# Sums of squares by one-column products in PSUM, and ScalarE scaling in the first layer's attention

## The chip, the core and the metric

The kernel runs on one core of a Trainium2 chip. A core has five engines that run side by side, each through its own queue in order: TensorE (PE, matrix products into PSUM), VectorE (DVE), ScalarE (ACT), GpSimd (POOL) and SyncE (SP, which here issues transfers). The metric is the device time of one execution in microseconds, as a median of several.

## What is computed

A decoder trunk of two layers on 512 prompt tokens and 8 sequences of 4 new tokens, all in float32, 544 columns in all. Cut to what matters here:

```
h  = rms_norm(x) * (1 + scale1(c)) + shift1(c)     # mean of squares over 1024 features
q  = rotary(rms_norm(q by heads)); k likewise      # mean of squares over 64 features of a head
p  = exp(s - m) / (sum exp(s - m) + exp(sink - m)) # attention in a window of 128, with sinks
o  = concat(rms_norm(o_attn), rms_norm(o_ssm), rms_norm(o_lru)) @ w_o
x  = x + gate1(c) * o
h2 = rms_norm(x) * (1 + scale2(c)) + shift2(c)
x  = x + gate2(c) * ConvFFN(h2)
```

The scales, shifts and gates come from c by a product with w_ada, a matrix of 1024 by 6144 for each layer.

## The kernel before

Features lie on the 128 partitions (1024 features are 8 chunks), tokens on the columns, and the columns are worked in two halves: half 0 has tokens 0 to 255, half 1 tokens 256 to 511 and the 32 new ones. A scheduler orders each engine's instructions at build time: in the order of the program, but what it reckons to be ready earlier may go first. `tc.keep_in_program_order` ties one instruction behind the one written before it on its engine.

**Stages.** The head (to about 66 us of the trace) loads x and the weights, computes the modulation and the first norm. Each layer then has mixers (to about 300 us, and from 700 to 933) and a feed-forward stage. In the head and the mixers, slabs of w_ada of 512 KB arrive through three buffers `raw`, which the weights share; PE multiplies each slab (L524, eight passes) and so sets its buffer free for the next transfer that SP has in its queue. Weights come through the same buffers, are split by ACT (`whi`, L415) and DVE (`wlo`, L416), and are multiplied in three passes (L430). Between these products PE takes small ones for attention, SSM and LRU, which ticks of hand-written generators interleave.

**Norms.** A norm needs, for every token, a sum of squares over features, that is over partitions and chunks. ACT squares the chunks; `sq_accum` adds them on DVE into one tile `sqacc` (L837). `mean_rstd` transposes it on PE in two blocks of 128 tokens (L459), so that tokens lie on partitions, and DVE reduces the columns (L465); the new tokens are summed by a product with a matrix of ones (L463). `rstd_small` takes the parts, scales each (L385), and finds the inverse root in eight further steps on DVE. `spread` transposes the result back to all partitions (L478), ACT copies it (L845), and the chunks are multiplied by it (L856). The head calls `sq_accum` for half 0 before its first slab and for half 1 before its ninth (`SQN`), and the statistics after two and after twelve slabs (`S12`), each pinned in PE's order.

The norms at the ends of stages have their squares added as the chunks come out of the residual. `head_rstd` does the same for each of five tiles of q and k in a layer: four transpositions (L931), a reduction over groups of 64 columns (L933), and a product with a block matrix of ones, `bones` (L936). `out_norm` adds two tiles of squares for SSM and LRU (L1126) before the same steps. The tiles of squares come from four buffers `half`.

**Attention.** A unit is one pair of heads by 128 queries, 16 units in a layer. `att_S` copies the sinks into the tile of scores (L1241), multiplies q and k (L1242), masks and finds the maximum (L1244), ACT takes exponentials with their sum, DVE the reciprocal (L1251) and scales two tiles of 256 or 128 columns (L384). PE transposes the result (L1263) and multiplies it by v (L1277).

Of the kernel before, what the change touches and what calls it, by code (L numbers as in the profile page):

```python
# [316 lines left out]
def trunk(ctx: ExitStack, tc: tile.TileContext, A, O):  # L317
# [130 lines left out]
    def mean_rstd(hfs, n, squares, pin=False):  # L448


        nb = 2 * len(hfs)
        m = nb + (32 if 1 in hfs else 0)
        c = sp.tile([128, 4], F32, tag="cs", name="cs", bufs=2)
        parts, held = [c[:, 0:nb]], []
        for i, hf in enumerate(hfs):
            sq = squares(hf)
            ps = one(256 + 32 * hf)
            for j in range(2):
                z = T_.transpose(ps[:, 128 * j:128 * j + 128], sq[:, 128 * j:128 * j + 128], eye)  # L459
                if pin and not i and not j:  # L460
                    tc.keep_in_program_order(z)
            if hf:
                T_.matmul(ps[:, 256:288], ones, sq[:, 256:288], start=False, stop=True, skip_group_check=True)  # L463
                parts.append(ps[:, 256:288])
            V.tensor_reduce(c[:, 2 * i:2 * i + 2], ps[:, 0:256].rearrange("p (j n) -> p j n", j=2),  # L465
                            axis=AX.X, op=OP.add)
            held.append(ps)
        r = sp.tile([128, 40], F32, tag="qr", name="qr", bufs=3)
        rstd_small(parts, n, r[:, 0:m])
        for ps in held:  # L470
            PS.put(ps)
        return r[:, 0:nb], r[:, nb:m]

    def spread(r, pin=False):
# [351 lines left out]

    SQ = {}

    def sq_accum(c, hf):
        a, b = HALF[hf]  # L830
        if c == 0:
            SQ[hf] = sp.tile([128, 288], F32, tag=f"sqacc{hf}", name="sqacc", bufs=1)[:, :b - a]
            act(SQ[hf], x[:, c, a:b], AF.Square)
        else:
            s = W(b - a)
            act(s, x[:, c, a:b], AF.Square)
            V.tensor_add(SQ[hf], SQ[hf], s)  # L837

    def norm_stats(hf, pin=False):

        r, rs = mean_rstd((hf,), 1024, lambda hf: SQ[hf], pin)
        yield
        ps = spread(r, pin)
        nr = SQ[hf]
        S.copy(nr[:, 0:256], ps)  # L845
        if hf:
            V.tensor_copy(nr[:, 256:288], rs)
        PS.put(ps)
# [77 lines left out]
            S.dma_start(dst[32 * i:32 * i + 32], src[o:o + 32])  # L926

    def head_rstd(M, sq):
        pt = one()
        for j in range(4):  # L930
            T_.transpose(pt[:, 128 * j:128 * j + 128], sq[:, 128 * j:128 * j + 128], eye)  # L931
        c = sp.tile([128, 8], F32, tag="ch", name="ch", bufs=2)
        V.tensor_reduce(c, pt.rearrange("p (n f) -> p n f", f=64), axis=AX.X, op=OP.add)  # L933
        PS.put(pt)
        pr = one(32)
        T_.matmul(pr, M.bones, sq[:, NP:NT], start=True, stop=True)  # L936
        r = sp.tile([128, 40], F32, tag="hr", name="hr", bufs=4)
        rstd_small((c, pr), 64, r)
        PS.put(pr)
        return r  # L940

    def k_chain(l, M, ps):
# [173 lines left out]
    def out_norm(l, M, os, at, n, hfs=(0, 1)):  # L1116
        d = LY[l]
        w = slice(HALF[hfs[0]][0], HALF[hfs[-1]][1])

        def squares(hf):  # L1120
            if not at:
                return M.sq.pop(hf)
            t = [W(HALF[hf][1] - HALF[hf][0]) for _ in os]
            for z, o in zip(t, os):
                act(z, o[:, slice(*HALF[hf])], AF.Square)
            V.tensor_add(t[0], t[0], t[1])  # L1126
            return t[0]

        r, rs = mean_rstd(hfs, n, squares)
        yield 1  # L1130
        nr = spread(r)
        a, b = w.start, min(w.stop, NP)
        for i, o in enumerate(os):
            wo = d["won"][at + i]
            stt(o[:, a:b], o[:, a:b], wo, nr, OP.mult, OP.mult)
            if 1 in hfs:
                stt(o[:, NP:NT], o[:, NP:NT], wo, rs, OP.mult, OP.mult)
        PS.put(nr)
        while not M.win_done:
            yield 1  # L1140
        for i, o in enumerate(os):
            split(o[:, w], [z[:, w] for z in hs[at + i]])
            M.o.update((at + i, hf) for hf in hfs)
            if at:
                free(o)
# [86 lines left out]
    def att_S(l, M, u):  # L1232
# [5 lines left out]
        pv = ps.rearrange("p (g n) -> p g n", g=2)  # L1238
        pm = M.pool.tile([128, 2, 257], F32, tag="pm", name="pm", bufs=PMB)
        st = sp.tile([128, 3, 2], F32, tag="st", name="st", bufs=4)  # L1240
        V.tensor_copy(pm[:, :, nk:nk + 1], d["nsink"][:, c, :, None])  # L1241
        T_.matmul(pv, M.q[c][:, j * 128:j * 128 + 128], M.kz[:, :, k0:k0 + nk], start=True, stop=True)  # L1242
        for g in range(2):
            V.tensor_tensor_reduce(out=pm[:, g, 0:nk], in0=pv[:, g], in1=M.maskp[:, 256 - nk:256],  # L1244
# [5 lines left out]
                accum_out=st[:, 1, g:g + 1])  # L1250
        V.reciprocal(st[:, 2], st[:, 1])  # L1251
        for g in range(2):
            ts(pm[:, g, 0:nk], pm[:, g, 0:nk], st[:, 2, g:g + 1])
        return pm

    def att_T(l, M, u, pm):
# [481 lines left out]
    for l in range(L):  # L1738
        with tc.tile_pool(name=f"mix{l}", bufs=1, reuse_waits="tile") as pool, ExitStack() as stack:
# [6 lines left out]
            if l == 0:  # L1746
# [13 lines left out]
                for n in range(24):  # L1760
                    if n == S3:
                        W_.ahead(GRP)
                        fetch_x(1)
                    for hf in range(2):
                        if n == SQN[hf]:
                            for c in range(KC):
                                sq_accum(c, hf)
                    for at, g in zip(S12, st + st):
                        if n == at:
                            next(g, None)  # L1770
# [41 lines left out]
```

## Time and profile before

| what | value |
|---|---|
| median of 3 runs | 1332.7 us (1332.39 to 1332.75) |
| the profiled execution | 1335.0 us, its span 1333.2 us |
| TensorE's granted clock, mean | 0.992 of full |
| PE busy | 1270.1 us, 10438 instructions |
| DVE busy | 881.8 us, 2583 instructions |
| ACT busy | 576.5 us, 1112 instructions |
| read from HBM | 159.37 MB |

The span runs from the first to the last instruction on record; the time of the execution includes what lies around it. PE's busy time counts overlapping passes once and is modelled at its ends. In the rows, L463 is line 463; `out<-in` names what is written and read; `x8` counts instructions; what stands in brackets is the engine's idle time before the row and what ended it.

### The profile page before, as it was taken

What the parts mean: (1) busy time and instruction counts of PE and PEld (TensorE: products, weight loads), DVE (VectorE), ACT (ScalarE), POOL (GpSimd) and SP (SyncE); (2) the same over time, 40 slices, a digit from 0 to 9 for tenths busy, and PEclk for the clock granted to TensorE, in tenths of its full rate; (3) what the DMA queues carried; (4) which work ended last, traced back from release to release, by engine and by line L of the source; (5) the groups of instructions that cost most, each with busy time, mean ns of one, the idle gap of its engine ahead of it and who ended that gap; (6) DMA issues with size and microseconds to landing.
All of it is one profiled execution on the core that took longest, in us unless ns stands there. A gap on an engine that the chain in (4) does not pass through costs nothing.

```text
span 1333.2 us, 26368 instructions
## 1 busy us (share of the span) xinstructions
PE 1270.1 (95%) x10438; PEld 1164.8 (87%) x10438; DVE 881.8 (66%) x2583; ACT 576.5 (43%) x1112; POOL 48.8 (4%) x82
## 2 busy tenths in 40 slices
PE   4899988999999999999999999899999999999998
PEld 2666765799999999999998776679999999999998
DVE  8787885988774556456576877668865456545651
ACT  4557544356542343234354466545643234313430
POOL 0021010000020000000000001000000000000000
PEclk9899999999999999999999999999999999999999
DMA  8876677533343223334235846602322332233221
GB/s 294 279 265 215 191 252 229 178 111 118 93 135 125 85 86 87 97 93 115 76 108 180 268 142 203 191 14 90 110 81 86 96 95 74 86 97 94 85 72 51
DMA packets 72460, 178.24 MB, mean 134 GB/s; under 512 B 15584, under 2 KB 26752, under 8 KB 72336
## 3 DMA queue, kind: packets, MB, share of 16 engines
q1 hardware_dynamic: 65456, 162.08, 39.1%
q0 software_dynamic: 4960, 11.68, 2.5%
q10 hardware_dynamic: 1920, 2.79, 0.7%
q8 instruction: 82, 1.34, 0.4%
q14 instruction: 42, 0.34, 0.1%
HBM read 159.37 MB, written 14.34 MB: 130 GB/s over the span
## 4 chain that ended last, share of the span: by engine, by line
PE 83%; DMA 9%; DVE 5%; ACT 2%; issue 1%; POOL 0%; SPq 0%; DVEq 0%; POOLq 0%; ACTq 0%
PE wide L430 42%; PE fb1w L430 9%; PE fb0w L430 8%; DMA raw<-in_wada_dram 6%; PE fb0s L430 5%; PE fb1s L430 4%; PE mb0s L430 3%; PE mb1s L430 3%; PE mb0s L524 1%; PE mb1s L524 1%; DMA raw<-in_wo_dram 1%; DVE wlo L416 1%; DMA f<-in_ssmh_dram 1%; DMA tab_br<-f 1%; PE mb1s L1242 0%
## 5 line engine op out<-in xcount | busy, mean ns | idle before, releaser
L430 PE MATMUL wide<-hh,whi 128*128 128x288 f32 (+1 forms) x1360 | 400.3, 295 | 1.2 <-ACT hh L897 0.8
L430 PE MATMUL wide<-hl,whi 128*128 128x288 f32 (+1 forms) x1360 | 395.9, 291 | 0.0
L430 PE MATMUL wide<-hh,wlo 128*128 128x288 f32 (+1 forms) x1360 | 394.3, 290 | 0.0
L416 DVE TENSOR_TENSOR wlo<-raw,whi 128x1024 fp32r<-128x1024 f32 (+1 forms) x176 | 211.0, 1200 | 187.1 <-ACT whi L415 183.1
L415 ACT CAST whi<-raw 128x1024 fp32r<-128x1024 f32 (+1 forms) x176 | 180.4, 1029 | 274.8 <-PE wide L430 125.8
L430 PEld LDWEIGHTS wide<-hh,whi 128*128 128x128 f32 x1360 | 257.2, 189 | 18.3 <-issue 14.0
L430 PEld LDWEIGHTS wide<-hl,whi 128*128 128x128 f32 x1360 | 257.1, 189 | 6.3 <-issue 6.1
L430 PEld LDWEIGHTS wide<-hh,wlo 128*128 128x128 f32 x1360 | 259.2, 191 | 3.0 <-issue 3.0
L380 DVE SCALAR_TENSOR_TENSOR f<-wide,prm,f 128x511 f32<-128x511 f32 x236 | 100.2, 485 | 0.0
L430 PE MATMUL wide<-mid,whi 128*128 128x256 f32 (+1 forms) x526 | 99.8, 287 | 0.0
L430 PEld LDWEIGHTS wide<-mid,whi 128*128 128x128 f32 x526 | 82.4, 188 | 0.0
L897 ACT CAST mid<-f 128x544 fp32r<-128x544 f32 x44 | 28.5, 647 | 122.4 <-DVE f L1660 119.1
L430 PE MATMUL wide<-mid,wlo 128*128 128x256 f32 (+1 forms) x263 | 75.5, 287 | 0.0
L377 ACT ACTIVATE f<-f 128x544 f32<-128x544 f32 x50 | 33.0, 659 | 89.2 <-DVE f L1650 84.5
L430 PE MATMUL fb1w<-hh,whi 128*128 128x256 f32 (+1 forms) x240 | 69.4, 289 | 1.8 <-ACT hh L862 1.3
L430 PE MATMUL fb1w<-hl,whi 128*128 128x256 f32 (+1 forms) x240 | 69.4, 289 | 0.0
L430 PE MATMUL fb1w<-hh,wlo 128*128 128x256 f32 (+1 forms) x240 | 68.8, 287 | 0.0
L430 PE MATMUL fb0w<-hh,whi 128*128 128x256 f32 (+1 forms) x224 | 64.7, 289 | 1.6 <-ACT hh L862 1.1
L430 PE MATMUL fb0w<-hl,whi 128*128 128x256 f32 (+1 forms) x224 | 64.7, 289 | 0.0
L430 PE MATMUL fb0w<-hh,wlo 128*128 128x256 f32 (+1 forms) x224 | 64.3, 287 | 0.0
L430 PE MATMUL fb0s<-mid,whi 128*128 128x288 f32 (+1 forms) x326 | 62.9, 290 | 0.0
L430 PE MATMUL fb1s<-mid,whi 128*128 128x288 f32 (+1 forms) x308 | 59.1, 289 | 0.0
(612 smaller groups left out, 2542.2 us busy)
## 6 DMA issues: line engine op xcount, KB each, us to landing
raw<-in_wada_dram SPq DMA_DIRECT2D x92, 512.0 KB, 5.2
raw<-in_wup_dram SPq DMA_DIRECT2D x88, 512.0 KB, 3.5
raw<-in_wdn_dram SPq DMA_DIRECT2D x32, 448.0 KB, 3.3
raw<-in_win_dram SPq DMA_DIRECT2D x24, 512.0 KB, 4.2
raw<-in_wo_dram SPq DMA_DIRECT2D x16, 512.0 KB, 4.5
raw<-in_wdn_dram SPq DMA_DIRECT2D x16, 512.0 KB, 3.5
e<-q ACTq DMA_DIRECT2D x32, 68.0 KB, 4.6
out_ox_dram<-x SPq DMA_DIRECT2D x8, 272.0 KB, 2.1
```

Of the source, the lines that this page charges most:

```text
L377: return S.activation(out, in_, f, bias=bias, scale=scale, **kw)
L380: return V.scalar_tensor_tensor(out, a, s, b, op0=op0, op1=op1, **kw)
L415: S.copy(hi, raw)
L416: V.tensor_sub(lo, raw, f32(hi))
L430: T_.matmul(out, w[wi][:, k, :], r[ri][:, a:b], start=first and i == 0, stop=last and i == 2)
L524: T_.matmul(ps[32 * g:32 * g + 32], silu[:, k, :], have[n][:, g], start=k == 0, stop=k == 7, skip_group_check=True)
L897: S.copy(dst[0], src)
```

## The change

Sums over features are now made by products in which the squares are the stationary operand and one column of ones moves; the result has tokens on partitions, as after a transposition, with the sum done. All products of a norm go into different columns of one PSUM tile and add up there, so several tiles of squares need no addition before. The first product of the tile clears it. In the head the squares are made when the norm asks for them (`sq_start`), one buffer each, and all eight chunks are multiplied; there is no `sq_accum` and no `SQN` in the head any more. The norms at the ends of stages still add their squares on DVE. `head_rstd` uses two columns of `bones` instead of a transposition and a reduction. In layer 0 alone, the copy of the sinks and the scaling of the probabilities are done on ACT.

```diff
@@ mean_rstd
-        c = sp.tile([128, 4], F32, tag="cs", name="cs", bufs=2)
-        parts, held = [c[:, 0:nb]], []
+        ps = one(m)
+        first = True
         for i, hf in enumerate(hfs):
-            sq = squares(hf)
-            ps = one(256 + 32 * hf)
-            for j in range(2):
-                z = T_.transpose(ps[:, 128 * j:128 * j + 128], sq[:, 128 * j:128 * j + 128], eye)
-                if pin and not i and not j:
-                    tc.keep_in_program_order(z)
-            if hf:
-                T_.matmul(ps[:, 256:288], ones, sq[:, 256:288], start=False, stop=True, skip_group_check=True)
-                parts.append(ps[:, 256:288])
-            V.tensor_reduce(c[:, 2 * i:2 * i + 2], ps[:, 0:256].rearrange("p (j n) -> p j n", j=2),
-                            axis=AX.X, op=OP.add)
-            held.append(ps)
+            for sq in squares(hf):
+                for j in range(2):
+                    z = T_.matmul(ps[:, 2 * i + j:2 * i + j + 1], sq[:, 128 * j:128 * j + 128], ones[:, 0:1],
+                                  start=first, stop=True, skip_group_check=True)
+                    if pin and first:
+                        tc.keep_in_program_order(z)
+                    first = False
+                if hf:
+                    T_.matmul(ps[:, nb:m], ones, sq[:, 256:288], start=False, stop=True, skip_group_check=True)
         r = sp.tile([128, 40], F32, tag="qr", name="qr", bufs=3)
-        rstd_small(parts, n, r[:, 0:m])
+        rstd_small([ps], n, r[:, 0:m])
@@ norms
+    def sq_start(hf):
+
+        a, b = HALF[hf]
+        SQ[hf] = sp.tile([128, 288], F32, tag=f"sqacc{hf}", name="sqacc", bufs=1)[:, :b - a]
+        for c in range(KC):
+            s = W(b - a)
+            act(s, x[:, c, a:b], AF.Square)
+            yield s
-        r, rs = mean_rstd((hf,), 1024, lambda hf: SQ[hf], pin)
+        r, rs = mean_rstd((hf,), 1024, lambda hf: [SQ[hf]] if hf in SQ else sq_start(hf), pin)
@@ head_rstd
-        pt = one()
+        ps = one(40)
         for j in range(4):
-            T_.transpose(pt[:, 128 * j:128 * j + 128], sq[:, 128 * j:128 * j + 128], eye)
-        c = sp.tile([128, 8], F32, tag="ch", name="ch", bufs=2)
-        V.tensor_reduce(c, pt.rearrange("p (n f) -> p n f", f=64), axis=AX.X, op=OP.add)
-        pr = one(32)
-        T_.matmul(pr, M.bones, sq[:, NP:NT], start=True, stop=True)
+            T_.matmul(ps[:, 2 * j:2 * j + 2], sq[:, 128 * j:128 * j + 128], M.bones[:, 0:128:64],
+                      start=j == 0, stop=True, skip_group_check=True)
+        T_.matmul(ps[:, 8:40], M.bones, sq[:, NP:NT], start=False, stop=True, skip_group_check=True)
-        rstd_small((c, pr), 64, r)
+        rstd_small([ps], 64, r)
@@ out_norm, squares
-                return M.sq.pop(hf)
+                return [M.sq.pop(hf)]
-            V.tensor_add(t[0], t[0], t[1])
-            return t[0]
+            return t
@@ att_S
-        V.tensor_copy(pm[:, :, nk:nk + 1], d["nsink"][:, c, :, None])
+        (V.tensor_copy if l else S.copy)(pm[:, :, nk:nk + 1], d["nsink"][:, c, :, None])
-            ts(pm[:, g, 0:nk], pm[:, g, 0:nk], st[:, 2, g:g + 1])
+            z = pm[:, g, 0:nk]
+            if l:
+                ts(z, z, st[:, 2, g:g + 1])
+            else:
+                act(z, z, AF.Copy, scale=st[:, 2, g:g + 1])
@@ the head
-                    for hf in range(2):
-                        if n == SQN[hf]:
-                            for c in range(KC):
-                                sq_accum(c, hf)
```

## Rows read from the trace of the kernel before

**Rows 1.** Busy time of each engine by stretch, clock, DMA share, GB/s.

```profile
66.00:133.00 67.00, 61.65 (x534) 45.77 (x527) 53.89 (x220) 43.70 (x102) 13.55 (x24) 1.00 0.74 238
...
500.00:600.00 100.00, 100.00 (x801) 100.00 (x801) 54.53 (x110) 30.88 (x47) 0.00 (x0) 1.00 0.31 92
700.00:890.00 190.00, 175.19 (x1497) 136.17 (x1496) 139.56 (x470) 103.20 (x234) 9.47 (x12) 0.99 0.57 175
```

**Rows 2.** The page: busy time of the engines; chain of waits by engine.

```profile
PE 1270.1 (95%) x10438; PEld 1164.8 (87%) x10438; DVE 881.8 (66%) x2583; ACT 576.5 (43%) x1112; POOL 48.8 (4%) x82
...
PE 83%; DMA 9%; DVE 5%; ACT 2%; issue 1%; POOL 0%; SPq 0%; DVEq 0%; POOLq 0%; ACTq 0%
```

**Rows 3.** Chain of waits from 66 to 262 us, shares by line.

```profile
by line: PE wide L430 19.0%; DMA raw<-in_wada_dram 17.8%; PE mb0s L524 7.5%; DMA raw<-in_wo_dram 7.1%; PE mb0s L430 6.3%; DMA f<-in_ssmh_dram 4.4%; DMA tab_br<-f 3.5%; PE mb0s L1081 2.7%; PE mb0s L1263 2.2%; PE mb0s L1242 2.2%; issue 2.1%; 
```

**Rows 4.** One piece of that chain in the head: start, us.

```profile
8.68 0.41 DVE sqacc L837
```

**Rows 5.** PE's timeline, three slabs of w_ada: start, us, [idle before].

```profile
13.94 1.08 PE L524 MATMUL wide<-raw,cin 128*32 128x256 f32 x8 [1.10 <-DMA raw<-in_wada_dram]
...
39.91 0.67 PE L524 MATMUL mb0s<-raw,cin 128*32 128x256 f32 x8 [1.30 <-DMA raw<-in_wada_dram]
42.06 1.08 PE L524 MATMUL mb0s<-raw,cin 128*32 128x256 f32 x8 [1.48 <-DMA raw<-in_wada_dram]
```

**Rows 6.** Busy time by stretch within the head; columns as in rows 1.

```profile
10.00:20.00 10.00, 7.01 (x67) 2.36 (x68) 9.90 (x113) 0.77 (x3) 0.00 (x0) 1.00 0.96 313
...
38.00:42.00 4.00, 1.28 (x16) 0.63 (x12) 2.44 (x13) 0.00 (x0) 0.54 (x1) 0.80 1.02 387
42.00:46.00 4.00, 3.48 (x22) 1.62 (x22) 1.80 (x8) 1.68 (x4) 0.00 (x0) 0.50 0.74 253
```

**Rows 7.** Timeline of the loads of weights on PE.

```profile
38.03 0.20 PEld L459 LDWEIGHTS mb0s<-eye,sqacc 128*128 128x128 f32 x2 [0.20 <-issue]
38.20 0.30 PEld L463 LDWEIGHTS mb0s<-sqacc,ones 128*128 128x128 f32 x2
...
44.39 0.33 PEld L430 LDWEIGHTS wide<-hl,whi 128*128 128x128 f32 x1
44.60 0.33 PEld L430 LDWEIGHTS wide<-hh,wlo 128*128 128x128 f32 x1
```

**Rows 8.** Line 463: duration ns min/median/max, first and last start.

```profile
L463 PEld LDWEIGHTS mb0s<-sqacc,ones x2: 190/191/192, 38.2 to 38.3; 128*128 128x128 f32 x2
```

**Rows 9.** Lines asked one by one: DVE operations, columns as in rows 8.

```profile
L837 DVE TENSOR_TENSOR sqacc<-sqacc,half x56: 417/438/459, 6.6 to 932.1; 128x256 f32<-128x256 f32 x28, 128x288 f32<-128x288 f32 x28
...
L465 DVE TENSOR_REDUCE cs<-mb1s x7: 415/425/425, 703.2 to 915.8; 128x2 f32<-128x256 f32 x7
...
L933 DVE TENSOR_REDUCE ch<-mb1s x5: 687/692/692, 769.1 to 851.3; 128x8 f32<-128x512 f32 x5
...
L1241 DVE COPY pm<-nsink x32: 106/164/170, 4.2 to 880.9; 128x2 f32<-128x2 f32 x32
...
L384 DVE TENSOR_SCALAR pm<-pm,st x64: 280/348/354, 94.3 to 891.0; 128x256 f32<-128x256 f32 x48, 128x128 f32<-128x128 f32 x16
...
L385 DVE TENSOR_SCALAR rst<-ch x10: 163/168/172, 69.3 to 852.0; 128x8 f32<-128x8 f32 x10
```

**Rows 10.** Groups on ACT, 66 to 243 us: busy us, mean ns.

```profile
L415 ACT CAST whi<-raw 128x1024 fp32r<-128x1024 f32 x11 | 11.5, 1048 | 12.6 <-DMA e<-e 4.7 <-DMA raw<-in_wo_dram 3.3 <-PE wide L430 3.0
...
L377 ACT ACTIVATE f<-f,gm 128x256 f32<-128x256 f32 x12 | 5.3, 499 | 0.7 <-DVE f L580 0.7
```

**Rows 11.** Who waited for lines 384 and 1126: us, times.

```profile
  PE mb0s L1263: 3.8, 3
...
  PE mb0s L459: 1.1, 2
```

**Rows 12.** Chain of waits at the end of the first mixers.

```profile
302.00 0.29 PE fb0s L478 x2
...
304.69 0.40 PE fb0w L430
```

More of the change, by code (lines that the diff above doesn't have):

```diff
@@ L452, in mean_rstd @@
         m = nb + (32 if 1 in hfs else 0)
-        c = sp.tile([128, 4], F32, tag="cs", name="cs", bufs=2)
-        parts, held = [c[:, 0:nb]], []
+        ps = one(m)
+        first = True
         for i, hf in enumerate(hfs):
-            sq = squares(hf)
-            ps = one(256 + 32 * hf)
-            for j in range(2):
-                z = T_.transpose(ps[:, 128 * j:128 * j + 128], sq[:, 128 * j:128 * j + 128], eye)
-                if pin and not i and not j:
-                    tc.keep_in_program_order(z)
-            if hf:
-                T_.matmul(ps[:, 256:288], ones, sq[:, 256:288], start=False, stop=True, skip_group_check=True)
-                parts.append(ps[:, 256:288])
-            V.tensor_reduce(c[:, 2 * i:2 * i + 2], ps[:, 0:256].rearrange("p (j n) -> p j n", j=2),
-                            axis=AX.X, op=OP.add)
-            held.append(ps)
+            for sq in squares(hf):
[7 more added lines that the diff above has]
+                    T_.matmul(ps[:, nb:m], ones, sq[:, 256:288], start=False, stop=True, skip_group_check=True)
         r = sp.tile([128, 40], F32, tag="qr", name="qr", bufs=3)
-        rstd_small(parts, n, r[:, 0:m])
-        for ps in held:
-            PS.put(ps)
+        rstd_small([ps], n, r[:, 0:m])
+        PS.put(ps)
         return r[:, 0:nb], r[:, nb:m]
@@ L928, in head_rstd @@
     def head_rstd(M, sq):
-        pt = one()
+        ps = one(40)
         for j in range(4):
-            T_.transpose(pt[:, 128 * j:128 * j + 128], sq[:, 128 * j:128 * j + 128], eye)
-        c = sp.tile([128, 8], F32, tag="ch", name="ch", bufs=2)
-        V.tensor_reduce(c, pt.rearrange("p (n f) -> p n f", f=64), axis=AX.X, op=OP.add)
-        PS.put(pt)
-        pr = one(32)
-        T_.matmul(pr, M.bones, sq[:, NP:NT], start=True, stop=True)
+            T_.matmul(ps[:, 2 * j:2 * j + 2], sq[:, 128 * j:128 * j + 128], M.bones[:, 0:128:64],
+                      start=j == 0, stop=True, skip_group_check=True)
+        T_.matmul(ps[:, 8:40], M.bones, sq[:, NP:NT], start=False, stop=True, skip_group_check=True)
         r = sp.tile([128, 40], F32, tag="hr", name="hr", bufs=4)
-        rstd_small((c, pr), 64, r)
-        PS.put(pr)
+        rstd_small([ps], 64, r)
+        PS.put(ps)
         return r
```

## The prediction

> **What bounds the kernel now.** Three views, from coarse to fine. First the busy time by stretch [rows 1]: in the feed-forward stage (500 to 600 us) PE is busy for all of 100 us and DVE for half. No edit touches that stage, and nothing can be won there. In the mixers of the first layer (66 to 133) PE is at 61.7 of 67 us, DVE at 53.9, ACT at 43.7; in those of the second (700 to 890) PE 175 of 190, DVE 140. There the engines wait for one another in turns, and there the edits lie, with the head (0 to 66 us) as the third place.
>
> Second, the chain of waits. Over the whole span PE owns 83% of it and DVE 5%, though DVE is busy 66% of the time [rows 2]. In the stretch 66 to 262 the PE lines named come to about 40% and DMA to a third; DVE has no line among the first [rows 3]. So a microsecond taken from DVE seldom shows at the end; one put on PE often does.
>
> Third, the head. The chain runs over DVE's additions of squares, as at 8.68 us [rows 4]. PE takes the w_ada slabs in order, as they land: it idled 1.10 us before the slab at 13.94, 1.30 before that at 39.91 and 1.48 before that at 42.06 [rows 5]. Eight passes over a slab took 0.67 us at 39.91 and 1.08 at 42.06, where the granted clock was 0.50 [rows 5, 6], the lower of the two levels (1.2 GHz). The slab at 13.94 also took 1.08, so I take the first stretch to have run at the lower level too, although its clock row says 1.00.
>
> **The price of a new product.** A product of float32 tiles is two passes, a transposition one: the product with ones at 38.20 shows two loads, two transpositions one each [rows 7]. One column instead of 128 shortens the streaming, not the load of the 128 columns of squares. A load takes 0.19 us and two take 0.30 together [rows 7, 8], so 0.11 us a pass; at the lower level successive loads start 0.21 apart (44.39, 44.60). The trace has no one-column product; below lies the possibility that its pass costs less than its load, above 0.21. I take 0.11 where the clock is 1.00, since it is the load that is seen.
>
> The Trainium skill (TensorE: Matmul & The Clock Gate, Back-to-back issue gap) lists about 60 cycles for a matmul of 1 to 64 columns, an estimate of 25 ns at the upper level. By that the 80 passes of the head cost 2.0 us and not 8.8; the row with two loads in 0.30 us speaks against it, and that page itself counts a load apart, by its columns.
>
> **Part by part: DVE.** Durations are from [rows 9]. Gone are 14 additions in the head at 0.44 us (6.1), 8 more of the same shapes in the output norms of SSM and LRU (3.5), 20 reductions at 0.42 (8.4), 10 reductions over 512 columns at 0.69 (6.9), and 20 small scalings at 0.17 (3.4), because all sums now stand in one PSUM tile. In layer 0, 16 copies at 0.16 and 32 scalings (24 at 0.35, 8 at 0.28) leave, 13.2. Sum 41.5: head 7.1, first mixers 22.3, second mixers 9.1, three later norms 3.0.
>
> **PE.** Head: 16 + 24 products, 80 passes for 6, +74. Each mixer: five head norms +4, SSM and LRU +14 each (two tiles are multiplied instead of one), the attention norm +4, so 52. Three later norms +4 each. In all 190 passes or 20.9 us: head 8.1, mixers 5.7 each, norms 1.3.
>
> **ACT.** 32 scalings of 128x256. The nearest row, a copy scaled by a column, is 0.50 [rows 10]: 16.0 us at most. The 16 copies of two columns: between 0.16 (DVE's) and 0.50, taken as 0.20: 3.2. No square is added; those of the head only move behind the norm's place in the order.
>
> **The sum, head.** (a) The additions and the reduction that lay on the chain go: about -1.5 us. (b) Half 0: 32 passes at 0.21 are 6.8 us, between two slabs. PE was busy 7.0 of 10 us there [rows 6], so 3.0 are hidden; of the 3.8 left, part delays the release of the slab buffers, whose DMA has share 0.96. Bounds 0 and +3.8, taken +2.0. (c) Half 1: 48 passes are 5.3 us at 0.11, ahead of the slabs at 39.91 and 42.06, which had 2.8 us of idle before them: +2.5. Against that, PE is then busy where it was idle and the clock stood at 0.80 and 0.50 [rows 6]; if it stays at 1.00, three slabs save 0.4 each and some 20 products up to 0.1 each (0.21 against a load's 0.11), -3.0. Bounds -0.5 and, all at the lower level (10.2 - 2.8), +7.4; taken -0.5. Eight squares share four buffers with other work; the fifth on ACT now waits for PE's products, and what stands behind it in ACT's queue (the copy of the spread statistics) waits for these too, so that costs nothing. Head: 0.0.
>
> **First mixers.** PE stood still 3.8 us, in three waits, for scaled probabilities and 1.1 us for the sum of two squares [rows 11]: 4.9. ACT's pair takes 1.0 us where DVE's took 0.7, so the three waits for probabilities keep 0.3 each: -4.0 (none, if ACT is late, to -4.9). The rest of DVE's relief: 22.3 times the 7% of its busy time that the chain shows (5% over a busy share of 66% [rows 2]): -1.6. The passes: 5.7 us on a PE that waits 8% of the time; from 0 (all in the gaps) to 2.3 (PE's 40% of the chain), taken +1.7, nearer the second since the gaps are scattered. Sum -3.9.
>
> **Second mixers.** DVE -0.6, passes +1.7: +1.1. **Three norms at the ends of stages.** PE ran out of products at 302.3 and had the next at 304.7 [rows 12]; the statistics come 0.59 us earlier (reduction and scaling) less 0.2 for two passes. Only if the products behind fill what is gained does it show: between -0.6 and +0.2 each, taken -0.3, -0.9.
>
> Total 0.0 - 3.9 + 1.1 - 0.9 = -3.7. The profiled execution took 1335.0 (span 1333.2, 1.8 around it) and gives 1331.3; it lay 2.3 above the median of the three runs, 1332.7. I apply the difference to the median: **1329.0 us**.
>
> **Rivals.**
>
> *Nothing shows at the end.* The slabs of w_ada and PE's order set the pace of the mixers; the passes eat what DVE gives. For it: a third of the chain on DMA [rows 3]. Against it: the 4.9 us of waits behind operations that leave. Price: the -5.6 of DVE's part in the first mixers falls to -2.8. Time 1332, within 1330.1 and 1335.3.
>
> *The sums hold up the slabs (slower).* PE takes its queue in order, so slabs wait behind 32 and 48 passes. If these run at the lower level, half 1 costs +7.4 instead of -0.5: -3.7 + 7.9 = +4.2, 1336.9. It decides once the head loses over 6.4 us. For it: the level of the clock before 33 us and after 40. Against it: the passes themselves keep PE at work.
>
> *ACT becomes the bound in the first mixers (slower).* ACT there goes up by 19 us, and a scaling stands behind casts of weights of 1.05 us [rows 10]. If a cast lies before the pair in half of 16 units and half of that is not covered, +4.2, and the -4.0 is gone: 1332.7 + 4.5 = 1337.2. For it: the exponentials that the scaling follows stand in the same queue. Against it: ACT was free for 23 of 67 us.
>
> For this rival the Trainium skill (ScalarE: Activation LUTs, Rules for kernel authors) says to multiply on VectorE and not on ScalarE; its 280 ns + 0.833 ns per element is an estimate of 0.49 us for 256 columns. The rows agree that ACT is the dearer place (0.50 against 0.35); whether the queue on DVE costs more than this, the page doesn't say.
>
> **How the numbers follow.** A difference under 0.2% (2.7 us) is about what a measurement of this kernel can't tell from none. Forecast 0.47 (some 1324 to 1330, all faster), nothing shows 0.23 (same), slabs held up 0.19 and ACT the bound 0.11 (slower). Below, the range takes in half 0 at no cost (-2.0), all 4.9 of the waits (-0.9), passes in the gaps (-3.4) and norms at -0.6 each (-0.9): 1321.8, and one microsecond and a half more for an order that falls better. Above, it takes in both slower rivals up to 1338. Range 1320 to 1338; the forecast's own is 1324 to 1330.
>
> **What would show it.** Right: at 38 us 48 passes at 0.11 us apart and the granted clock above 0.9 from 38 to 50; the waits of the transpositions of probabilities for DVE gone, with none as large for ACT; DVE busy near 840. Wrong: passes 0.21 apart there and slabs starting 5 us later than 39.9 and 42.1; transpositions that wait for ACT's scaling by over 4 us in sum; the end of the second mixers later against its start by more than 2 us, which would mean that the passes all lie on the path.

## The result and the profile after

The changed kernel is slower: a median of 1367.05 us over 4 runs (1362.65 to 1370.85), against 1332.72 of the kernel before on the same chip. The ratio is 1.0257, 95% interval 1.0223 to 1.0290, some 34 us. The forecast was 1329.0, and the range ended at 1338.

The profiled execution took 1365.33 us, its span 1363.5, with a mean granted clock of 0.975 (0.992 before). The engines' busy times and the chain by engine, from the page of the changed kernel:

```profile
PE 1314.7 (96%) x10628; PEld 1205.6 (88%) x10628; DVE 853.2 (63%) x2463; ACT 597.1 (44%) x1166; POOL 48.7 (4%) x82
PE 88%; DMA 6%; DVE 3%; ACT 2%; issue 1%; SPq 0%; ACTq 0%; POOL 0%; DVEq 0%; POOLq 0%
```

Against [rows 2]: the counts of the forecast hold. PE has exactly 190 instructions more. ACT is 20.6 us busier, near the 19.2 expected, but by luck: 7.7 of it are loads of function tables that the forecast did not count (last section), and the scaling and the copies alone, in a run described below, made ACT 12.8 us busier (589.3 against 576.5). DVE is 28.6 us less busy, not 41.5; the durations of its single operations do sum to 39.7 less, but operations in a row overlap, and busy time counts the overlap once. The relief shows nowhere at the end: PE's share of the chain went up.

Where the time went is read from the 176 casts of weights on ACT, which come in the order in which the weights are used. The table gives the start of the n-th in the profiled execution of before, and how many microseconds later it is in that of seven others (the runs are described below):

```
cast   stage                      before    after  head  head    scaling  passes  passes  one pass,
no.                                                alone undone  undone   added,  added,  squares
                                                                          head    mixers  added
  1    head, half 0                 22.4      5.0   5.1   0.5      5.4     2.8     0.1     1.4
  4    head, half 1                 50.4      9.8  10.1   0.5     13.2     9.0    -1.1     1.7
 10    first mixers                 85.8     10.1  10.0  -1.1     14.4     8.3    -1.1     1.3
 11    first mixers                 96.5     24.4  11.9   5.9     18.2     8.7    -0.7     1.5
 17    first mixers                186.3     14.2   7.1  -5.1     16.1     6.5    -6.6     0.6
 19    late in the first mixers    261.9     27.8   8.3   9.2     21.8     8.7    -0.9     7.8
 91    end of feed-forward         688.1     28.7   8.3  10.0     22.7     8.7    -0.5     8.2
111    late in second mixers       918.5     30.3   5.7  21.2     24.1    11.5     5.0    10.1
176    second feed-forward        1292.5     30.3   5.5  21.2     24.1    11.3     4.9    10.2
```

In the changed kernel 10 us are lost in the head, 18 more in the first mixers, and under 2 in the second, in this one execution of each. The feed-forward stages pass the loss on unchanged.

**The head.** Three rows of PE's timeline before, which the argument compares with (the second is the first product with a weight, the third spreads the statistics of half 1):

```profile
22.60 0.69 PE L536 MATMUL mb0s<-eye,half 128*128 128x128 f32 x2 [0.55 <-ACT half L531]
27.50 0.58 PE L430 MATMUL mb0s<-hh,whi 128*128 128x256 f32 x1 [4.21 <-ACT hh L862]
...
43.07 0.69 PE L478 MATMUL wide<-eye,qr 128*128 128x128 f32 x2
```

PE's timeline of the changed kernel (start, length, engine, line and operation, count, idle time before); the products with one column are L458, the sums of the new tokens L464, the slabs L520, the statistics spread by transposition L474:

```profile
11.32 4.43 PE L458 MATMUL wide<-ones,half 128*128 128x1 f32 x20
...
27.65 0.54 PE L532 MATMUL mb0s<-eye,half 128*128 128x128 f32 x2 [0.55 <-ACT half L527]
33.54 0.58 PE L430 MATMUL mb0s<-hh,whi 128*128 128x256 f32 x1 [5.35 <-ACT hh L867]
...
44.68 0.61 PE L458 MATMUL mb0s<-ones,half 128*128 128x1 f32 x4
45.15 0.39 PE L464 MATMUL mb0s<-half,ones 128*128 128x32 f32 x2
45.37 0.58 PE L458 MATMUL mb0s<-ones,half 128*128 128x1 f32 x4
...
49.03 0.99 PE L458 MATMUL mb0s<-ones,half 128*128 128x1 f32 x4
49.88 0.61 PE L464 MATMUL mb0s<-half,ones 128*128 128x32 f32 x2
50.43 1.06 PE L520 MATMUL mb0s<-raw,cin 128*32 128x256 f32 x2
51.42 1.01 PE L458 MATMUL mb0s<-ones,half 128*128 128x1 f32 x4
52.30 0.61 PE L464 MATMUL mb0s<-half,ones 128*128 128x32 f32 x2
52.84 1.93 PE L520 MATMUL mb0s<-raw,cin 128*32 128x256 f32 x14
55.02 0.69 PE L474 MATMUL wide<-eye,qr 128*128 128x128 f32 x2 [0.25 <-DVE qr L380]
```

The reader is to see four things. The first product with a weight starts at 33.54 where it was 27.50. The slab that stood at 39.91 [rows 5] begins at 50.43 with two of its eight passes; the other six and the eight of the next slab (42.06 before) run from 52.84 on. The six passes for one square of half 1 are four at L458 and two at L464: they take 0.69 us from 44.68 to the next square's, which start at 45.37, 0.11 each, and 1.40 from 49.03 to the slab that follows, more than 0.21 each. And between these two the clock fell, with PE busy all the time. The windows of that stretch (length, then busy time of PE, PEld, DVE, ACT and POOL, the granted clock, the DMA share and GB/s):

```profile
45.00:48.00 3.00, 3.00 (x29) 3.00 (x28) 0.00 (x0) 1.69 (x4) 0.00 (x0) 1.00 0.85 321
48.00:51.00 3.00, 3.00 (x16) 2.54 (x15) 0.00 (x0) 0.08 (x1) 0.00 (x0) 0.56 0.00 1
51.00:54.00 3.00, 3.00 (x19) 1.94 (x20) 0.91 (x5) 0.00 (x0) 0.00 (x0) 0.50 0.00 0
54.00:57.00 3.00, 2.75 (x17) 0.84 (x12) 1.86 (x9) 0.72 (x2) 0.00 (x0) 0.50 0.62 205
```

PE was busy for 3.00 of 3.00 us and yet ran at the lower level (1.2 GHz), and for six microseconds no byte moved: the slabs' buffers were full and stood behind the sums in PE's queue. The waits of the queue that issues transfers, 42 to 60 us:

```profile
SPq L503 <- PE mb0s L520: 12.0, 3, 7.7
```

**The first mixers.** PE's waits between 66 and 290 us in the changed kernel, where the stage ends later (what waited, for what: us in total, times, longest):

```profile
PE mb0s L520 <- DMA raw<-in_wada_dram: 4.8, 5, 1.5
PE wide L936 <- ACT e L377: 2.1, 1, 2.1
PE mb0s L1268 <- ACT pm L377: 1.8, 1, 1.8
```

The waits of [rows 11] for DVE are gone, as forecast; in their place the transpositions of probabilities (L1268) wait 1.8 us for ACT, where the forecast left 0.9. All waits of PE in that stretch sum to 12.4 us; before they were 17.2, up to 262. PE waits less and the stage takes 18 us longer: the time is in PE's own work. The windows between the starts of casts 10 and 19, before and after (columns as above):

```profile
85.80:261.90 176.10, 161.53 (x1445) 118.33 (x1444) 139.08 (x572) 93.64 (x226) 15.74 (x25) 0.98 0.68 215
```

```profile
95.90:289.70 193.80, 183.28 (x1497) 135.70 (x1495) 123.40 (x490) 114.89 (x279) 16.20 (x25) 0.90 0.63 196
```

PE is idle for 10.5 us instead of 14.6 and busy for 21.8 us more, with 52 passes more, which are 5.7 us at 0.11. The clock's record has PE at the lower level for 37.5 us of this stretch, before for 6.8. PE is busy through nearly all of it, so half of the difference of 30.7 is work not done: 15.4 us. The two make up 21.1 of the 21.8.

### The profile page after: what moved, and what is told of

Same layout as the page of the kernel before. It is cut to its first block, busy times and chain, and to the rows that moved or that the text cites. A ratio compares the mean times of both kernels' runs of the same rounds, so it can differ in the third digit from the quotient of the medians.

```text
span 1363.5 us, 26669 instructions
## 1 busy us (share of the span) xinstructions
PE 1314.7 (96%) x10628; PEld 1205.6 (88%) x10628; DVE 853.2 (63%) x2463; ACT 597.1 (44%) x1166; POOL 48.7 (4%) x82
## 4 chain that ended last, share of the span: by engine, by line
PE 88%; DMA 6%; DVE 3%; ACT 2%; issue 1%; SPq 0%; ACTq 0%; POOL 0%; DVEq 0%; POOLq 0%
PE wide L430 42%; PE fb1w L430 8%; PE fb0w L430 8%; PE fb0s L430 5%; PE fb1s L430 4%; DMA raw<-in_wada_dram 4%; PE mb1s L430 3%; PE mb0s L430 3%; PE mb0s L520 2%; PE mb1s L520 1%; PE wide L520 1%; PE wide L458 1%; DVE wlo L416 1%; PE mb0s L1282 1%; PE mb0s L458 1%
## 5 line engine op out<-in xcount | busy, mean ns | idle before, releaser
L430 PEld LDWEIGHTS wide<-hh,whi 128*128 128x128 f32 x1360 | 258.5, 190 | 14.5 <-issue 12.8
```

Of the source, the lines that this page charges most:

```text
L430: T_.matmul(out, w[wi][:, k, :], r[ri][:, a:b], start=first and i == 0, stop=last and i == 2)
```

## The experiments

All ran beside the kernel before on the same chip; its medians there lay between 1332.3 and 1332.8. Ratios are to those runs, with 95% intervals. Single executions of one kernel scatter by up to 13 us to either side of its median, so a profiled execution is used for where something happens, and the ratio for how much.

**1. The edits one at a time.** The head alone:

```
 def norm_stats(hf, pin=False):
-    r, rs = mean_rstd((hf,), 1024, lambda hf: SQ[hf], pin)
+    if hf in SQ:
+        r, rs = mean_rstd((hf,), 1024, lambda hf: SQ[hf], pin)
+    else:
+        r, rs = mean_cols((hf,), 1024, sq_start, pin)
```

> Before, with the head's edit alone: eight squares of each half multiplied by ones on PE as they come, nothing added on DVE; head norms, output norms, later norms and the scaling of probabilities as before. Theory A (the head loses it: in a PE queue that is taken in order, squares in four buffers and slabs of w_ada hold one another up): the first product with a weight of half 0 starts at 33 us and that of half 1 at 56, as in the changed kernel (27.5 and 44.2 before), and the time rises by at least 10 us, to 1343 or more; if the head alone carries the whole loss, to 1360. Theory B (the scaling on ScalarE loses it, the late head is caught up behind the slabs): within 5 us of before, 1328 to 1338.

Measured: 1342.62 us, 1.0090 (1.0057 to 1.0123). The head costs 10 us, so the part of theory A on the head holds, but it is a third of the loss. The changed kernel with the head's squares added on DVE again:

```
 if n == S3:
     W_.ahead(GRP)
     fetch_x(1)
+for hf in range(2):
+    if n == SQN[hf]:
+        for c in range(KC):
+            sq_accum(c, hf)
```

> The changed kernel with the head's squares added on DVE again; the sums there go by one-column products over the one added tile. Theory A: the loss goes, 1326 to 1338. Theory B: the loss of the mixers stays, 1350 or more.

Measured: 1353.42, 1.0147 (1.0105 to 1.0188). Theory A falls as a whole: 20 us are lost without the head. The scaling alone (with the copy of the sinks, which its edit also moves to ACT), and everything but these two:

```
-ts(pm[:, g, 0:nk], pm[:, g, 0:nk], st[:, 2, g:g + 1])
+z = pm[:, g, 0:nk]
+if l:
+    ts(z, z, st[:, 2, g:g + 1])
+else:
+    act(z, z, AF.Copy, scale=st[:, 2, g:g + 1])
```

> Before, with the probabilities of the first layer scaled on ScalarE (and the sink copied there) and nothing else changed. Theory A: 1326 to 1335, and PE's waits for scaled probabilities in the stretch 66 to 262 us (3.8 us before) fall to about 1. Theory B: 1345 or more, and PE or DVE wait on ScalarE's scalings for over 4 us in sum.

> The changed kernel with the probabilities scaled on DVE again, the sums by products with ones as changed. Theory A: the loss stays, 1355 to 1372. Theory B: it falls by over 12 us, under 1353.

Measured: 1332.01 for the scaling alone, 0.9998 (0.9974 to 1.0021), and 1358.15 for all but the scaling, 1.0188 (1.0149 to 1.0226). Theory B falls with the first. The waits of PE from 66 to 262 us in the run with the scaling alone:

```profile
PE mb0s L524 <- DMA raw<-in_wada_dram: 11.2, 8, 4.2
PE mb0s L914 <- ACT g L377: 1.0, 1, 1.0
PE wide L524 <- DVE rst L385: 0.7, 1, 0.7
```

The 3.8 us of waits for scaled probabilities [rows 11] are gone, and none for ACT's stand in their place. PE waits for the next slab of w_ada instead, 11.2 us where it was 8.6. So the slabs' transfers took back 2.6 of the 3.8 us. The rest is not waiting: between casts 10 and 19 PE is idle for 12.6 us instead of 14.6, but busy for 164.3 instead of 161.5 with as many instructions, and the clock was at the lower level for 13.7 us instead of 6.8. So this execution gained nothing. Its row for that stretch:

```profile
84.10:261.00 176.90, 164.29 (x1443) 119.60 (x1441) 130.07 (x525) 106.31 (x272) 15.72 (x25) 0.96 0.68 214
```

**2. The sums of the mixers, apart.**

```
 f2: mean_rstd as changed, head_rstd, head's squares and scaling as before
 f4: only
-    T_.transpose(pt[:, 128 * j:128 * j + 128], sq[:, 128 * j:128 * j + 128], eye)
+    T_.matmul(ps[:, 2 * j:2 * j + 2], sq[:, 128 * j:128 * j + 128], M.bones[:, 0:128:64], ...)
```

> Before, with the sums of squares of attention, SSM, LRU and the later layer norms by one-column products; the head's squares added on DVE, the norms of the q and k heads and the scaling as before. With the head's edit undone the changed kernel took 20.9 us more than before, and the scaling alone nothing. Theory E (the output norms, whose two square tiles are now held to the products): 1345 or more. Theory F (the norms of the heads, which PE takes too early in its queue and for which it stood 5.8 us): within 5 us of before, 1328 to 1338.

> Before, with the norms of the q and k heads alone by products with the two columns of the block of ones, four for the prompt's tiles. Theory E: within 5 us of before, 1328 to 1338. Theory F: 1345 or more, with a wait of PE for the square of k of over 4 us between 185 and 200 us.

Measured: 1338.25 for the output norms, 1.0061 (1.0038 to 1.0084), and 1338.43 for the norms of the heads, 1.0048 (1.0026 to 1.0069). Neither theory holds: each costs 6 to 8 us, and no single edit carries the loss. The wait of over 4 us for the square of k that theory F asks for did not come either: with the norms of the heads alone PE's longest wait for ACT from 185 to 262 us is 0.4 us. The parts (0.9, 0.6, 0.5 and 0%) sum to 2.0%, the whole is 2.57%.

**3. What the head pays for.** Wider products, more buffers, half the passes, and the passes alone:

```
 f1: the head alone, ones[:, 0:1]  ->  ones[:, 0:64]
 f3: the head alone, s = W(b - a)  ->  s = W(b - a) if c < 4 else E(b - a)
 h2: f1 with  act(s.bitcast(F32R), x[:, c, a:b], AF.Square)  and ones.bitcast(F32R)
 h4: the kernel before, and behind its transpositions
+for k in range(8):
+    for j in range(2):
+        T_.matmul(ps[:, 320 + 2 * k + j:321 + 2 * k + j], sq[:, 128 * j:128 * j + 128], ones[:, 0:1], ...)
+    if hf and k < 7:
+        T_.matmul(ps[:, 352:384], ones, sq[:, 256:288], ...)
```

> The run with the head's edit alone, its sums by products with 64 columns of ones where there was one; the first of the 64 is used. Theory C (a stretch of one-column products counts for little work, so that the granted clock falls behind it, as at 47 us): the 13.7 us at the lower level from 47 us on go or shrink to under 5, and the time falls by 4 us or more, to 1338 or less. Theory D (the waits of PE and the order of its queue make the clock fall, the width of the products does not matter): the clock falls there as before and the time is within 3 us of 1342.6.

Measured: 1340.30, 1.0061 (1.0039 to 1.0083). In its profiled execution, 5 us under its median, all 48 passes of half 1 ran at 0.11 us and the clock did not fall there, and casts 4 and 10 came 4.4 and 0.8 us late instead of 10.1 and 10.0: as many passes cost next to nothing at the end of the head where the clock held; but in the run of all sums with 64 columns (4, below) it fell at 44 us, just behind the first of them, for 13.7 us. The intervals of one and of 64 columns overlap, and so does the clock: the median over all executions is 0.987 for both. So theory C is not shown for the head. Half 0 of this run, for the price of a pass:

```profile
11.48 7.09 PE L484 MATMUL wide<-ones,half 128*128 128x64 f32 x32
```

> The run with the head's edit alone, with eight buffers for its squares instead of four (the last four squares of a half in the four tiles that the mixers use later). Theory G (four buffers tie ScalarE's squares to PE's queue and the squares, the products and the slabs wait for one another): the products of half 0 are done by 16 us instead of 21, the first product with a weight starts at 29 to 30 us instead of 33.5, and the time falls by 5 us or more, to 1337 or less. Theory H (it is the passes and their place ahead of the slabs): the start moves by less than 2 us and the time stays within 3 us of 1342.6.

Measured: 1340.88, 1.0073 (1.0047 to 1.0098). Half 0's sums were done at 18.5 us where the changed kernel ended them at 21.5, and the first cast of weights came 2.9 us late instead of 5.1; then the sums of half 1 stood before the slabs as ever, and cast 4 was 11.8 late. The buffers are worth 2 us in half 0 and nothing at the end. Theory G falls.

> The kernel before with nothing taken away: behind the two transpositions of each half's added square stand as many one-column products as the head's edit has, on the added square, into columns that nobody reads (16 for half 0; 23 for half 1). No square waits for PE, no buffer is held, DVE does all its additions. Theory I: 1338 or more, and the first product with a weight starts 5 us later for half 0 and 9 to 12 later for half 1. Theory G: within 3 us of before.

Measured: 1346.94, 1.0101 (1.0071 to 1.0131): as much as the whole edit of the head, with no square waiting and DVE doing all its work. PE's timeline of it:

```profile
11.88 6.83 PE L465 MATMUL wide<-ones,sqacc 128*128 128x1 f32 x32
...
44.96 0.58 PE L465 MATMUL mb0s<-ones,sqacc 128*128 128x1 f32 x4
45.41 0.39 PE L468 MATMUL mb0s<-sqacc,ones 128*128 128x32 f32 x2
45.63 0.83 PE L465 MATMUL mb0s<-ones,sqacc 128*128 128x1 f32 x4
46.33 0.61 PE L468 MATMUL mb0s<-sqacc,ones 128*128 128x32 f32 x2
...
49.43 1.94 PE L531 MATMUL mb0s<-raw,cin 128*32 128x256 f32 x16
```

The first product with a weight starts 4.5 us late (32.00), that of half 1 9.0 (53.20 for 44.22). The same picture: 0.21 us a pass in half 0, 0.11 at first in half 1, 0.21 behind 46 us, and the two slabs back to back behind them.

> The head's edit alone, with 64 columns and the squares in the short form, one pass for each product: 40 passes in place of 80, four buffers as before; the squares are rounded. Theory I (the passes on PE cost the time, at 0.21 us each where the clock is low): the first product with a weight starts within 1 us of before (27.5), and the time is 1333 to 1338, at least 4 us under the 1342.6 and 1340.3 of two passes. Theory G (four buffers tie the engines together): 1339 or more.

Measured: 1335.59, 1.0020 (1.0001 to 1.0039), with half 0 and half 1 of it here:

```profile
11.49 3.20 PE L486 MATMUL wide<-ones,half 128*128 128x64 f32 x14
...
22.87 0.44 PE L560 MATMUL mb0s<-eye,half 128*128 128x128 f32 x2 [0.55 <-ACT half L555]
...
40.61 0.41 PE L486 MATMUL mb0s<-ones,half 128*128 128x64 f32 x2
...
45.19 2.77 PE L548 MATMUL mb0s<-raw,cin 128*32 128x256 f32 x18
```

The transposition that stood at 22.60 before stands at 22.87, and half 1's sums end at 45. With half the passes, the same buffers and the same relief of DVE, three quarters of the head's loss are gone; against the run with 64 columns and two passes, from which it differs in the passes and the rounding of the squares alone, two thirds, with intervals that meet at 1.0039. The clock is no better: 0.985 at the median. For the head theory I is shown by this run and the one before it together: it is the passes. That their cost hangs on the clock that they meet is what the execution with 64 columns suggests.

**4. Width and passes in all sums.**

```
 g1: the changed kernel, 64 columns in every sum; heads M.bones[:, 32:96]
 g2: f2 with 64 columns
 g3: g1, squares of head, SSM and LRU in the short form, one pass
 g4: g3 with the head's squares added on DVE
 h1: g1 with the scaling on DVE
 h3: g2 with one pass for SSM and LRU
```

> The changed kernel with 64 columns of ones (or of the block of ones) in every product of the sums where there were one or two; two passes each as before, and the first column of each 64 is used. Theory C (stretches of one-column products let the clock fall): the granted clock of the run rises from 0.975 to 0.985 or more, no stretch of 10 us at the lower level follows on products of sums, and the time falls by 10 us or more, to 1357 or less. Theory I (the 190 passes cost their price on PE whatever their width): 1362 to 1372.

> The run with the output norms' sums alone, with 64 columns. It fell to the lower level for 10.2 us at 234 us, behind 3 us of one-column products. Theory C: that stretch goes, and the time falls from 1338 to 1334 or less. Theory I: within 2 us of 1338.

> The run with 64 columns in every sum, with the squares of the head, of SSM and of LRU written in the short form that PE multiplies in one pass: 80 passes of the head and about 90 of the mixers become half as many; the squares are rounded. Theory I: 8 to 12 us less than with two passes. Theory C: within 4 us of it, since the passes no longer matter once the clock holds.

> The same with the head's squares added on DVE: sums of SSM and LRU in one pass with 64 columns, the norms of q and k heads with 64 columns in two passes, probabilities scaled on ScalarE. The kernel with this head and one-column products took 1353.4. Theory C: 1330 to 1338. Theory I: 85 passes of two kinds fewer than that, 1340 to 1346. A version that beats the kernel before would be under 1329.

Measured: all with 64 columns 1351.35, 1.0136 (1.0105 to 1.0166); the output norms alone 1339.20, 1.0047 (1.0021 to 1.0073); all in one pass 1345.75, 1.0102 (1.0074 to 1.0131); that with the head undone 1331.83, 1.0004 (0.9980 to 1.0028). Width gained 16 us over the changed kernel, as theory C has it, with as many instructions on PE (10628), and the lower level between 66 and 300 us fell from 41.0 to 17.1; but the clock came up to 0.983 only, and in the single parts width gained nothing that can be told: the output norms have a clock of 0.992 with it and 0.989 without, and the same time. One pass gained 5.6 more, fewer than theory I has and with intervals that overlap, and undoing the head another 14. The expectations count too many passes saved: by PE's instructions (10548 and 10518) all in one pass has 80 fewer than with two, and the version with the head undone has 40 fewer than 10558 with one column, not 85. These 40 are 8.4 us at 0.21 and it gained 22 us: passes are not all of it.

> The changed kernel with 64 columns in every sum (18 us over before) and the probabilities scaled on DVE again. The scaling on ScalarE alone cost nothing, but the changed kernel without it took 9 us less than with it, on another chip. Theory J (ScalarE's scalings do cost beside the other edits, where weight casts on ScalarE are already late): 1344 or less, 7 us below. Theory K (the 9 us are the difference between chips and orders): within 3 us of 1351, and the cast of weights at 96 us of before is as late without the scaling as with it.

> The output norms' sums alone, with 64 columns and one pass a product for SSM and LRU; as many passes there as the transpositions and sums of before had, within 10. Theory I: the 6 us that two passes cost (with 1 or 64 columns) go, 1330 to 1335. Theory L (the two square tiles held for PE, or the order that comes of it, cost it): 1337 or more.

Measured: 1347.69, 1.0102 (1.0063 to 1.0141), without the scaling, which overlaps the run with it: neither J nor K is shown. Its cast 11 came 4.9 us late, against 20.8 with the scaling, which speaks against K; but its profiled execution took 1334.74 with 20.5 us at the lower level, 13 us under its own median. The output norms in one pass took 1335.29, 1.0016 (0.9994 to 1.0038): in theory I's range, with half of their added passes gone (40 more than before by PE's instructions, not within 10 as the expectation has it, and 80 with two passes); but the intervals of one pass and of two with 64 columns overlap.

**5. Passes without relief in the mixers, and relief without passes.**

```
 i1: the kernel before, in each norm of the mixers and each later layer norm
+for k in range(0 if pin else more[hf]):
+    T_.matmul(ps[:, 300 + k:301 + k], sq[:, 0:128], ones[:, 0:1], ...)
 i2: squares added on DVE as before, the last sum in the short form; then one pass with
     64 columns in place of transposition and reduction
```

> The kernel before with nothing taken away and 116 one-column passes added: 4 in each norm of q and k heads, 14 in each norm of SSM and LRU, 4 in that of attention and in each later layer norm, into columns that nobody reads; as many as the change adds behind the head. Theory I (passes cost all of their price in the mixers of both layers, 0.11 to 0.21 us each): 1345 to 1357. Theory M (the mixers' loss comes from the order that the edits bring about, from squares held or from norms waited for, and the passes themselves fit into gaps): 1330 to 1339. DVE does here all the work that the change takes from it: the difference to 1353.4 of the run with the head undone is what that relief was worth.

> Squares added on DVE everywhere as before; in place of the transpositions and reductions, products with 64 columns of ones in one pass (the added square is rounded); heads' norms and scaling as before. PE has some passes fewer than before, DVE 8 us less. Theory I: 1329 to 1334, on either side of before by less than can be told. A gain of over 3 us would mean that DVE's reductions did lie on the path.

Measured: 1339.83 with the 116 passes, 1.0040 (1.0016 to 1.0065), between the two theories. In its profiled execution the stretch between casts 10 and 19 takes 176.1 us, as before: with 41 passes more there PE is busy for 4.3 us more and idle for as much less, so they fitted into the gaps, and the loss comes in the second mixers (5.0 at cast 111). The run with the head undone, with nearly as many passes, all the relief in the mixers and the scaling, lost 20.9 us: the relief gave nothing that shows.

With the squares added on DVE and one pass it is 1342.25, 1.0084 (1.0054 to 1.0114). PE has not fewer instructions than before, as the expectation says, but exactly as many, 10438; DVE is 5.8 us less busy. This is against theory I: with no pass more it is 10 us slower. Its loss lies between casts 17 and 19. There PE stands in its queue at a norm of the k heads before ACT has squared k. The place before, in that run, and in the run with the head undone:

```profile
197.26 1.01 PE L931 MATMUL wide<-eye,e 128*128 128x128 f32 x4
```

```profile
196.93 0.69 PE L943 MATMUL wide<-eye,e 128*128 128x128 f32 x2 [3.54 <-ACT e L377]
```

```profile
196.81 1.87 PE L936 MATMUL wide<-bones,e 128*128 128x2 f32 x8 [5.79 <-ACT e L377]
```

In the run with the head undone ACT was itself in front of a weight's cast that waited for its transfer (first its row, then the run's windows around it):

```profile
194.59 1.04 ACT L415 CAST whi<-raw 128x1024 fp32r<-128x1024 f32 x1 [5.26 <-DMA raw<-in_wo_dram]
```

```profile
190.00:200.00 10.00, 4.21 (x22) 3.98 (x23) 5.71 (x14) 3.51 (x7) 1.40 (x2) 0.65 0.66 207
200.00:210.00 10.00, 9.97 (x102) 6.90 (x102) 5.98 (x29) 1.69 (x4) 0.71 (x1) 0.67 0.46 119
```

Before, PE met that norm at 197.26 us behind other work and did not wait for ACT. With the head undone it stood still for 5.8 us, and the clock was at the lower level for 13.7 us from 193 on. The order in which PE takes its work is remade with every edit, here as in the changed kernel (2.1 us of wait at L936, and 10.2 at the lower level from 212 on).

## Why the prediction was wrong

**The head (0.0 forecast, 10 us measured).** The step that failed is (c), half 1, taken at -0.5 because PE would be kept busy and the clock would stay at 1.00. It fell at 48 us, in the midst of the products, with PE at 3.00 of 3.00 us. The upper bound of that step, +7.4 with all passes at the lower level, was nearly the truth: from 33.54 (6.0 late) to 55.02 (11.9 late) half 1 added 6. In the one execution where the clock held, that with 64 columns, cast 10 was 0.8 late, near the forecast. Half 0 was taken at +2.0: as bare passes it does cost 1.9 (22.60 to 24.45 in the run with passes added), but in the edit 5.1. The other 3 go with the four buffers: from the fifth on, ACT's squares come one at a time, three of them after 0.44 us of waiting for PE, PE takes passes of slabs between their products (15.67 to 20.54), and the sums end at 21.5 instead of 18.7. The prediction put that wait at nothing; eight buffers take 2 of the 3 us away. The sign that it named, slabs 5 us later than 39.9 and 42.1, came as 10.5 and about 11.

**The price of a pass** held: 0.11 us at the upper level, 0.21 at the lower, with one column as with 64 (6.83 and 7.09 us for 32 in half 0, where the clock's rows say 1.00 but a slab takes 1.08 us, as it does at 0.50). By the Trainium skill (TensorE: Matmul & The Clock Gate, Back-to-back issue gap) an isolated matmul of up to 64 columns has an issue gap of some 60 cycles, an estimate of 25 ns at the upper level, and in a stream of loads and matmuls both set the spacing; the rows agree that a pass with its load takes more, 0.11 us. What was wrong was which level, and how much is hidden.

**First mixers (-3.9 forecast, +18 measured).** The larger step that failed is that the clock stays: the sum had no term for it outside the head, and between casts 10 and 19 PE was at the lower level for 30.7 us more, which cost it 15.4. The smaller one is the balance of relief and passes. The waits for DVE did go, and PE is idle for 4.1 us less; but its idle time fell as much (4.3) in the run with passes added and all of DVE's work kept. So the passes use up the gaps with the relief or without it, and the two together came to +1.6 (5.7 less 4.1) where the sum had -3.9. Which of the two terms was wrong the runs do not part.

**Second mixers (+1.1) and the later norms (-0.9)** came as +1.6 between casts 91 and 111 and +0.9 between 19 and 91, small either way in the changed kernel. That they are near is luck: with the head undone the second mixers lost 11.

**The rivals.** "The sums hold up the slabs" is what the head did, at 1342.6 instead of 1336.9. "ACT becomes the bound" did not come: ACT's scalings alone cost nothing. No case held all parts at once with a falling clock, so the range ended 29 us too low.

**What ties it together, and what stays open.** Over the 20 profiled executions, the time goes with the time that PE spent at the lower level: a correlation of 0.91, and 0.61 us for each microsecond there. Before it is 20.5 us, after 68.3; 47.8 times 0.61 gives 29 of the 30.3 us between these two executions. This is a bond and not a cause by itself, and the record of the clock in every execution weakens it: over the 115 executions of the kernel before that ran beside these, with between 11 and 51 us at the lower level, it is 0.18 us for each microsecond, at a correlation of 0.48. That a microsecond there costs less where PE has idle time to give would fit this; no run tests it. In the head the cause is shown: the passes bring it about; that the clock sets their price rests on one execution, that with 64 columns. In the mixers, where two thirds of the loss lie, it stays open. Four things go with it, and the runs do not part them: the passes (0.4% alone, and nothing in the first mixers), their width (16 us between one column and 64 in all sums, nothing in single parts), PE's standing at a norm whose square is late (the version with the squares added and one pass loses 0.8% with it, the norms of the heads alone lose 0.5% without it), and all of these beside the scaling. Why the clock falls within a stretch of short products in some executions and not in others is not settled. No version beat the kernel before; the scaling alone, the output norms in one pass and the version with the head undone in one pass cannot be told from it.

## What to carry to other kernels

A microsecond taken from an engine that the chain hardly names is worth nothing until it is known what waits next, and a microsecond put on the engine that the chain does name is paid, at the clock that it has there, wherever that engine has no gap left: the 78 passes added to the head cost 14 us, the 116 added to the mixers, 12.8 us at the least, cost 7.5. Count what an edit adds to PE in passes, price them at the lower level wherever the rows show it nearby, and look at what stands behind them in PE's queue: here the next slab and with it all transfers. A cheap way to know such a price beforehand is to add the passes and take nothing away; that the order stays the same has then to be looked at too, since here any edit remade it.

## What the runs showed of the hardware

A product with one column of ones takes PE as long as one with 64: 0.21 us a pass at the lower level and 0.11 at the upper. The granted clock fell while PE was busy without a gap, as at 48 us above and at 46 with passes added. And the loads of ACT's function tables, which the forecast had not counted, change with edits that move no function to ACT: 29 before and 35 after, from the groups of ACT (count, busy time, mean ns of one, idle time before); the third row is that of the head's edit alone:

```profile
L377 ACT ACT_TABLE_LOAD x29 | 37.2, 1283 | 5.5 <-DMA e<-q 3.1 <-issue 1.1 <-PEq L1801 0.8
```

```profile
L377 ACT ACT_TABLE_LOAD x35 | 44.9, 1283 | 4.2 <-DVE ex L380 2.0 <-DVE rst L441 1.0 <-PEq L1802 0.8
```

```profile
L377 ACT ACT_TABLE_LOAD x35 | 44.9, 1283 | 3.1 <-DVE rst L441 1.2 <-PEq L1831 0.8 <-issue 0.6
```

Six loads more are 7.7 us of ACT. They do not come from the scaling: with the scaling alone there were 29 again, and with all but the scaling 33. Nor do they explain the loss: the run with passes added to the head has 29 and loses as much as the head's edit with 35.
